# Spreading norms by transposes, and issuing 64-row products by turns, in a two-layer hybrid diffusion backbone

## The chip, the cores and the metric

The kernel runs on one core of one Trainium2 chip. The metric is the device time of one execution in microseconds (us), the median of the runs shown; lower is better. TensorE (PE) is the matrix engine, VectorE (DVE), ScalarE (ACT) and GpSimd (POOL) do the elementwise work, and SyncE (SP) issues the transfers. The profile is one execution taken by the hardware profiler.

## The reference, cut to what matters

Two layers; each is a feed-forward, a mixing sub-layer of two head groups (windowed attention and the RWKV-7 scan, run in both directions), and a second feed-forward. 512 latent tokens and 256 context tokens, 1024 channels, 8 + 8 heads of 64 channels, float32.

```python
def rms_norm(x, gain):
    xf = x.astype(jnp.float32)
    y = xf * lax.rsqrt(jnp.mean(xf * xf, axis=-1, keepdims=True) + RMS_EPS)
    return (y * gain.astype(jnp.float32)).astype(x.dtype)

def attn_heads(p, q_gain, k_gain):            # q and k: a norm per head
    q, k, v = jnp.split(p, 3, axis=-1)
    q = rms_norm(q.reshape(shape), q_gain) * ATTN_SCALE
    k = rms_norm(k.reshape(shape), k_gain)
    ...
def neighbourhood_attention(q, k, v, k_ctx, v_ctx, rel_bias):
    ...
        s_loc = jnp.einsum('bqhd,brwhd->bhqrw', q_i, k_i) + bias[None]
        s_ctx = jnp.einsum('bqhd,bchd->bhqc', q_i, k_ctx)
        p = jax.nn.softmax(jnp.concatenate([s_loc, s_ctx], axis=-1), axis=-1)
        # out = p_loc @ v_i + p_ctx @ v_ctx
def rwkv_prepare(p, ...):
    kk = heads(k * key_k)
    kk = kk * lax.rsqrt(jnp.maximum(jnp.sum(kk * kk, axis=-1, keepdims=True), L2_EPS))
    for d in range(2):
        w_log = -jax.nn.softplus(-(decay_w0[d] + jnp.tanh(dw) @ decay_w2[d])) - 0.5
        a = jax.nn.sigmoid(iclr_a0[d] + da @ iclr_a2[d])
        ...
# per layer: x += 0.5 g0 ffn(norm(x)); x += g1 mix(norm(x)); x += 0.5 g2 ffn(norm(x))
```

## The kernel before, in words

Channels lie on the 128 partitions, tokens along the free dimension. The feed-forwards (`up` L341, `accumulate` L423) are wide products on all 128 rows of TensorE. Each starts with `prep_end` (L283): the sums of squares of all tokens come out by tokens, and the reciprocal root (L294) is spread over the channels by six products of a broadcast column with the identity (L300), four tokens' tiles into one PSUM bank and two into a second; ACT copies each bank out as `rstd`.

The mixing sub-layer (`mix` L1096) is a set of streams, each a generator: the scan's chains, the solves, the blocks (`rwkv_blocks` with `rwkv_block` L780), the projections (`rkv` L655, `qkv` L469), in layer 0 the next layer's modulations (`mod` L170), the attentions (`attention` L515) and the output projection. `drive` (L71) takes their steps by turns: each `yield` gives a share of TensorE and a distance to the stream's next step, from the table `E` (L68). A planner then orders the instructions of each engine; it takes the ready one of the highest rank, and the ranks are chains, solves, blocks, then all the others, in the order in which `drive` issued them. On the chip each engine runs its instructions in that fixed order.

PSUM has eight banks, by tag (L65): two of `g` for the wide products and for the attention's scores and outputs, two of `p` for the RWKV preparation, two of `a` for the attention's transposes and the norms, one each for the chain and its outputs.

Per-head norms go through `head_rms` (L446), used for q, k and the scan's direction kk: the heads' sums (L451), a root and a reciprocal, a spreading along the free dimension on DVE (L460), and then four or six products with the identity (L465) that bring the result over the channels. DVE multiplies by it (L164, from L494 and L674).

`attention` takes a head pair: 6 blocks of 128 queries in layer 0 (the last two of the context), 4 in layer 1. A unit is one block and one head, and a head's 64 channels lie on one half of the rows. A step of the stream is the scores of unit n (L557, L560, or L542 for the context) into a `g` bank, DVE's evacuation with the bias and the maximum (L562), the exponential, and the transposes (L577, L575) of unit n - 2; after the second head of a block come the products with v (L598) and a copy out. So a head pair has 14 steps in layer 0 and 10 in layer 1. The score tiles have four places (tag `w2`).

In `rwkv_block`, run 12 times per layer, two lots of two 256-column products (L797) fill one `p` bank each: the decay's on rows 0 to 63, then the learning rate's on rows 64 to 127; ACT reads each bank through a tanh. The products `gt` (L856) of the preceding block use the same two banks.

Of the kernel before, what the change touches and what calls it, by code (L numbers as in the profile page):

```python
# [12 lines left out]
ALU = mybir.AluOpType  # L13
# [10 lines left out]
# half of the columns of the feed-forward's first product, even as the products ask for  # L24
# [4 lines left out]
# head pairs are scanned two at a time  # L29
# [10 lines left out]
# A chunk of 32 tokens of the RWKV scan is computed, per head and direction, on a state tile's columns X = [S; V; U] with S by channels,  # L40
# V and U by tokens, of its rows SR[e], VR[e] and UR[e], by a block of 128 columns: X's next S by channels, its outputs, and U from [S; V].
# A stage holds the blocks of a head pair's 4 chunks, by head, direction and chunk.
# [15 lines left out]
# SBUF tiles by tag: (floats per partition, tiles)  # L58
TAGS = dict(x=(2 * XH, 6), r=(2 * XH, 10), g3=(772, 3), z=(2 * XH, 3), k=(4 * XH, 2), sp=(520, 8), ob=(512, 4), ro=(256, 5),
            st=(SW, 8), w2=(512, 4), wr=(512, 3), q4=(1024, 3))  # L60
# The feed-forward's first product goes by Winograd's form of Strassen's algorithm: seven products of half the features, channels and tokens.
# The tags of the tiles that hold its right operands' 56 parts
PARTS = ("st",) * 3 + ("k",) * 2 + ("sp",) * 8 + ("ob",) * 4 + ("q4",) + ("z",) * 2 + ("x",) * 6 + ("r",) * 2
# PSUM banks by tag: GEMM, chain, chain's outputs, RWKV preparation, attention
BANKS = dict(g=2, ch=1, co=1, p=2, a=2)  # L65
OUTS = (0, 2, 4, 6)
# weights of the streams' steps (TensorE's share, distance to the stream's next step): they set the order of issue
# [3 lines left out]
def drive(tc, *streams):  # L71
    """Issues the steps of the streams, the first of them that is ready at a time, TensorE's use setting the clock.
    The scheduler prefers the streams in the order of their ranks."""
    now, live, first = 0.0, [[0.0, g, rank] for rank, g in streams], tc.cur_priority
    prio = {rank: first + rank * 200000 for rank, _ in streams}
    while live:
        for s in live:
            if s[0] > now:
                continue
            tc.cur_priority = prio[s[2]]  # L80
            step = next(s[1], "end")
            prio[s[2]] = tc.cur_priority
            if step == "end":
                live.remove(s)
                break
            if step is not None:
                s[0] = max(now + step[0], now + step[1])
                now += step[0]
                break
        else:  # L90
            now = max(now + 0.2, min((s[0] for s in live if s[0] > now), default=0.0))
    tc.cur_priority = max(prio.values())
# [14 lines left out]
class Net:  # L107
# [62 lines left out]
    def mod(self, l, i, tag, cols, bank):  # L170
# [3 lines left out]
        for c0 in range(0, KD * D, step):  # L174
# [6 lines left out]
            # the four column groups at once  # L181
# [71 lines left out]
    def prep_wino(self, kt, tag="g3"):  # L253
        """The right operands of k-tiles kt and kt + 4: x scaled, and twice the shifts."""
# [28 lines left out]
    def prep_end(self):  # L283
# [13 lines left out]
        for t0, hs in ((0, XLAT), (4, xctx))[:2 if self.prep_ctx else 1]:  # L297
            pb = self.bank("a", "rsps")
            for t in range((hs.stop - hs.start) // 128):
                nc.tensor.matmul(pb[:, 128 * t:128 * t + 128], lhsT=rs[:, t0 + t:t0 + t + 1].to_broadcast([128, 128]),  # L300
                                 rhs=self.c(C_ID), start=True, stop=True)
# [4 lines left out]
    def weight(self, src):  # L306
        """The parts of four tiles of weights: (high, low)."""
# [6 lines left out]
    def product(self, w, xh, xl, segs, banks="g"):  # L314
        """The product's segments one after the other: (columns, PSUM) as each is finished."""
# [25 lines left out]
    def up(self, raw, ctx, hh, hl):  # L341
        """A tile of the hidden features."""
# [80 lines left out]
    def accumulate(self, src, k0, n, hh, hl, ctx, gate, after, banks="g"):  # L423
        """Adds the gated product of input tiles k0 to k0 + n to x, two output tiles m and m + 4 at a time."""
# [13 lines left out]
    def residual(self, product, m, gate):  # L438
        """Adds the gated product to x."""
# [6 lines left out]
    def head_rms(self, sq, nt, mean, tag, bank):  # L446
        """1/sqrt of each head's sum (or mean) of squares, spread over that head's channels, in PSUM banks."""
# [14 lines left out]
        for t0 in range(0, nt, 4):  # L462
            pb = self.bank(bank, "hrb")
            for t in range(t0, min(t0 + 4, nt)):
                nc.tensor.matmul(pb[:, 128 * (t - t0):128 * (t - t0) + 128], lhsT=rs[:, 128 * t:128 * t + 128], rhs=self.c(C_ID), start=True, stop=True)  # L465
# [3 lines left out]
    def qkv(self, l, p, last):  # L469
        """q and k normalised, and v in the order of the windows' key groups, of head pair p, to DRAM."""  # L470
# [31 lines left out]
    def transposed_tiles(self, out, src):  # L502
        """The transposes of six tiles of 128 x 128."""
# [6 lines left out]
    # key groups of v by tokens, of 128: columns 8-23, 24-39, 40-55, 0-7 with 56-63 of all rows, then the context  # L510
    # of each block of 16 query columns: (first column, columns, groups of them, step) of its keys, and their groups of v (group, its first key)
# [3 lines left out]
    def attention(self, l, p, last):  # L515
# [10 lines left out]
        units = [(b, e) for b in range(4 if last else 6) for e in range(2)]  # L526
        nab, sbs, pbs = {}, {}, {}

        def slots(b):
            """(group of v, its keys, the first's column of the scores); blocks 4 and 5 are the context's."""  # L530
# [6 lines left out]
        def scores(b, e):  # L537
            rows = HALVES[e]
            nm = self.small("nm", [128, 1])
            if b > 3:  # L540
                ps = self.bank("g", "scc", (128, 256))
                nc.tensor.matmul(ps, lhsT=q[rows, 128 * b:128 * b + 128], rhs=k[rows, CTX], start=True, stop=True)  # L542
                nc.vector.tensor_reduce(out=nm, in_=ps, axis=AX.X, op=ALU.max, negate=True)
                sb = self.t("w2", "scs", 256)
                self.softmax(sb, ps, 1.0, nm)
                return sb
# [6 lines left out]
            ps = self.bank("g", "sc")  # L553
            lq = q[rows, 128 * b:128 * b + 128]
            o = 0
            for c0, n, g, step in self.KEYS[b]:
                nc.tensor.matmul(ps[:, o:o + 8 * n * g], lhsT=lq,  # L557
                                 rhs=free_ap(k[rows, c0:c0 + 1], [[step, g], [GW, 8], [1, n]]), start=True, stop=True)
                o += 8 * n * g
            nc.tensor.matmul(ps[:, 256:512], lhsT=lq, rhs=k[rows, CTX], start=True, stop=True)  # L560
            sb = self.t("w2", "sc", 512)
            nc.vector.tensor_tensor_reduce(out=sb.rearrange("p (a c) -> p a c", a=2),  # L562
                                           in0=ps.rearrange("p (a c) -> p a c", a=2),
                                           in1=free_ap(nab[y][:, e], [[256 * (2 - e), 2], [1, 256]]), scale=-1.0,
                                           scalar=3.0e38, op0=ALU.add, op1=ALU.min, accum_out=nm)
            self.softmax(sb, sb, -1.0, nm)
            return sb
# [18 lines left out]
        lag = 2  # L586
        for n in range(len(units) + lag):
            if n < len(units):
                sbs[units[n]] = scores(*units[n])
            if n >= lag:  # L590
                b, e = units[n - lag]
                pbs[e] = transposed(b, sbs.pop((b, e)))
                if e:
                    sl = slots(b)
                    pv = self.bank("g", "pv", (128, 128))
                    for s, (g, ks, _) in enumerate(sl):
                        for h, rows in enumerate(HALVES):
                            nc.tensor.matmul(pv[rows], lhsT=vt[ks, g, rows], rhs=pbs[h][ks, 128 * s:128 * s + 128],  # L598
                                             start=s == 0, stop=s == len(sl) - 1)
                    if b > 3:  # L600
                        self.act(out[:, 128 * b:128 * b + 128], pv, AF.Copy)
                    else:
                        self.act(out[:, LAT].rearrange("p (i b c) -> p b i c", b=4, c=16)[:, b], pv.rearrange("p (i c) -> p i c", c=16), AF.Copy)
            yield E["a"]
# [12 lines left out]
    def shifted(self, l, m, ctx):  # L617
        """Token-shifted projection tile m (14 of them), the context's tokens first: (tile, its column of token 0)."""
# [36 lines left out]
    def rkv(self, l, p, last):  # L655
        """r, k and k's direction of head pair p by blocks of 256 tokens, and v, to DRAM."""
# [40 lines left out]
    def span(b, d):  # L697
        """Tokens (context first) of block b of 256 in the order of direction d's scan."""
# [3 lines left out]
    def rwkv_bonus(self, l, p, b0, b1, g):  # L702
        """Sum over a head's channels of r (k_f + k_b) u, times v, of the blocks b0 to b1 of tokens."""
# [14 lines left out]
    def rwkv_blocks(self, l, i, last):  # L718
        """The blocks of group i of two head pairs, but for U's part in itself."""
# [26 lines left out]
    def rwkv_solves(self, l, i):  # L746
        """The inverses of group i, applied to the blocks' U rows."""
# [32 lines left out]
    def rwkv_block(self, l, p, b, emit, ltd, g):  # L780
        """Block b of 256 tokens of each direction's scan, with the backward direction's tokens reversed: two stages."""
# [9 lines left out]
        # tanh of half the decay's and of minus half the learning rate's argument  # L791
        th, tan = self.t("sp", "th", 512), self.t("sp", "tan", 512)
        for i, t in enumerate((th, tan)):
            rows = HALVES[i]
            ps = self.bank("p", "lz", (128, 2, 256))
            for d in range(2):
# [456 lines left out]
```

## Time and profile before

| | |
|---|---|
| median of 3 runs (3946.70, 3961.48, 3950.52) | 3950.52 us |
| span of the profiled execution | 3962.7 us |
| PE busy | 3659.5 us, 92% of the span |
| PE weight loads (beside PE) | 3152.3 us, 80% |
| DVE busy | 2934.9 us, 74% |
| ACT busy | 1498.9 us, 38% |
| POOL busy | 1005.3 us, 25% |
| mean granted TensorE clock | 0.926 of full speed |

The span is what the profiled execution took, 12.2 us (0.3%) over the median and 1.2 us over the longest of the three runs. A float32 product leaves two records on PE, a transpose one. Records of successive products overlap, so a merged row of n records is shorter than n times the time of one, and PE's busy time is the union of its records. A clock of 1.00 is 2.4 GHz, 0.50 is 1.2 GHz.

### The profile page before, as it was taken

The numbers are of one execution on the slowest core, as the hardware profiler recorded it, in microseconds if no ns is written. First come the engines' busy times: TensorE is split into PE (matmuls) and PEld (weight loads), VectorE is DVE, ScalarE is ACT, GpSimd is POOL, SyncE is SP. The second block draws the span as 40 slices with busy tenths as digits, with TensorE's granted clock in tenths as the row PEclk, the third lists the DMA queues.
The fourth block names the chain that finished last, engine by engine and source line by source line (L and its number), as shares of the span: only waits on it lengthen the run. The fifth ranks groups of instructions, "written<-read, shape, count | busy, mean of one in ns | idle before, by whom it ended". The sixth has DMA issues, their size and how long they took to land. (4 is left out here: it accounts for less than half of the span.)

```text
span 3962.7 us, 73554 instructions
## 1 busy us (share of the span) xinstructions
PE 3659.5 (92%) x28980; PEld 3152.3 (80%) x28980; DVE 2934.9 (74%) x5682; ACT 1498.9 (38%) x2968; POOL 1005.3 (25%) x1156
## 2 busy tenths in 40 slices
PE   6999999999799899799999999999998977878988
PEld 4788889878666567699998999998886756768888
DVE  5666678575868766788878888886668686768888
ACT  4232224343444432533335433334434442243333
POOL 2222222020312311322323322230203131133333
PEclk8999999989899779799999999999998885779999
DMA  5333332332245243111121111123322210212222
GB/s 194 123 118 108 107 107 73 102 95 76 69 151 173 90 150 111 66 67 64 65 75 54 65 64 67 66 71 115 108 88 73 68 60 18 70 59 94 82 82 94
DMA packets 229849, 354.62 MB, mean 89 GB/s; under 512 B 47744, under 2 KB 156672, under 8 KB 217216
## 3 DMA queue, kind: packets, MB, share of 16 engines
q1 hardware_dynamic: 229504, 349.92, 26.9%
q8 instruction: 229, 3.75, 0.4%
q14 instruction: 116, 0.95, 0.1%
HBM read 306.31 MB, written 43.52 MB: 88 GB/s over the span
## 5 line engine op out<-in xcount | busy, mean ns | idle before, releaser
L364 PE MATMUL mw<-b,wq 128*128 128x386 f32 (+1 forms) x4224 | 783.4, 329 | 15.5 <-ACT wq L167 9.0
L364 PEld LDWEIGHTS mw<-b,wq 128*128 128x128 f32 x4224 | 701.8, 191 | 40.4 <-ACT wq L167 11.6
L322 PE MATMUL mm<-h,whi 128*128 128x256 f32 (+1 forms) x2816 | 669.9, 331 | 22.1 <-ACT h L167 20.1
L164 DVE SCALAR_TENSOR_TENSOR x<-mm,mods,x 128x256 f32<-128x256 f32 (+1 forms) x768 | 418.0, 573 | 192.8 <-PE mm L322 188.8
L322 PEld LDWEIGHTS mm<-h,whi 128*128 128x128 f32 x2816 | 475.4, 191 | 99.0 <-ACT h L167 23.5
L364 PE MATMUL mw<-b,whi 128*128 128x386 f32 (+1 forms) x2112 | 520.6, 329 | 30.4 <-ACT b L167 11.8
L322 PE MATMUL mm<-h,wlo 128*128 128x256 f32 (+1 forms) x1408 | 450.2, 328 | 2.0 <-DVE wlo L161 1.9
L364 PEld LDWEIGHTS mw<-b,whi 128*128 128x128 f32 x2112 | 373.8, 190 | 40.3 <-ACT b L167 16.0
L167 ACT ACTIVATE whi<-wraw 128x512 fp32r<-128x512 f32 x312 | 196.1, 629 | 493.4 <-PE mm L322 297.1
L364 PE MATMUL mw<-b,wlo 128*128 128x386 f32 (+1 forms) x1056 | 346.6, 328 | 1.1 <-DVE wlo L161 0.8
L167 ACT ACTIVATE wq<-raw 128x512 fp32r<-128x512 f32 x352 | 219.6, 628 | 338.3 <-PE mw L364 264.7
L161 DVE TENSOR_TENSOR wq<-raw,wq 128x512 fp32r<-128x512 f32 x352 | 292.4, 832 | 68.2 <-ACT wq L167 65.3
L322 PEld LDWEIGHTS mm<-h,wlo 128*128 128x128 f32 x1408 | 268.6, 192 | 28.5 <-DVE wlo L161 2.8
L161 DVE TENSOR_TENSOR wlo<-wraw,whi 128x512 fp32r<-128x512 f32 x312 | 222.3, 714 | 54.1 <-ACT whi L167 38.0
L161 DVE TENSOR_TENSOR up_g<-up_g,mw 128x386 f32<-128x386 f32 (+1 forms) x352 | 182.3, 518 | 92.2 <-PE mw L364 75.5
L161 POOL TENSOR_TENSOR raw<-raw,s 128x512 f32<-128x512 f32 x88 | 125.7, 1428 | 432.1 <-DVE wq L161 429.5
L161 POOL TENSOR_TENSOR s<-raw 128x512 f32<-128x512 f32 x88 | 125.2, 1423 | 432.5 <-DVE wlo L161 371.4
L167 ACT ACTIVATE whi<-s 128x512 fp32r<-128x512 f32 x176 | 110.5, 629 | 321.0 <-PE mm L322 229.3
L322 PE MATMUL mm<-x,whi 128*128 128x258 f32 (+2 forms) x832 | 207.5, 335 | 0.0
L364 PEld LDWEIGHTS mw<-b,wlo 128*128 128x128 f32 x1056 | 201.1, 190 | 3.2 <-DVE wlo L161 2.4
L184 PE MATMUL modps<-wmod,cs 128*32 128x256 f32 x1152 | 172.7, 427 | 23.6 <-DMA wmod<-in_w_mod_dram 22.9
L161 POOL TENSOR_TENSOR up_g<-up_g,rstd 128x386 f32<-128x386 f32 (+1 forms) x88 | 103.5, 1176 | 342.8 <-DVE up_g L161 337.9
(226 smaller groups left out, 7043.5 us busy)
## 6 DMA issues: line engine op xcount, KB each, us to landing
raw<-in_ffn_up_dram SPq DMA_DIRECT2D x88, 1024.0 KB, 5.4
wraw<-in_ffn_down_dram SPq DMA_DIRECT2D x176, 256.0 KB, 3.1
wmod<-in_w_mod_dram SPq DMA_DIRECT2D x144, 256.0 KB, 3.1
wmod<-in_w_mod_dram SPq DMA_DIRECT2D x224, 128.0 KB, 2.2
wraw<-in_w_in_dram SPq DMA_DIRECT2D x104, 256.0 KB, 2.8
wmod<-in_w_mod_dram SPq DMA_DIRECT2D x8, 1024.0 KB, 10.9
wraw<-in_w_out_dram SPq DMA_DIRECT2D x32, 256.0 KB, 3.1
in<-rkv SPq DMA_DIRECT2D x20, 384.0 KB, 3.9
```

Of the source, the lines that this page charges most:

```text
L161: (eng or self.nc.vector).tensor_tensor(out=out, in0=a, in1=b, op=op)
L164: self.nc.vector.scalar_tensor_tensor(out=out, in0=a, scalar=s, in1=b, op0=op0, op1=op1)
L167: self.nc.scalar.activation(out, in_, f, **kw)
L184: nc.tensor.matmul(ps[q:q + 32], lhsT=self.cs[:, kt], rhs=w, start=kt == 0, stop=kt == KD - 1)
L322: nc.tensor.matmul(ps, lhsT=wt, rhs=xt[k][:, c0:c1], start=k == 0 and n == 0, stop=k == nk - 1 and n == 2)
L364: nc.tensor.matmul(ps, lhsT=wt[:, c], rhs=self.bs[i][k][xt], start=k == 0 and m == 0, stop=k == 3 and m == 2)
```

## The change

Three edits. The products with the identity that spread norms (L300, L465) become transposes of the same operand. In `attention` a step is now the scores of both heads of a block, with the matrix products by turns for the two halves of the rows, into both `g` banks; or the transposes of both heads of the preceding block with their products with v. A head pair has 12 steps in layer 0 and 8 in layer 1, of the same weights. In `rwkv_block` the four products with `lora` are issued by turns for the halves, so that both `p` banks are taken before the first tanh. Comments are dropped.

```diff
             for t in range((hs.stop - hs.start) // 128):
-                nc.tensor.matmul(pb[:, 128 * t:128 * t + 128], lhsT=rs[:, t0 + t:t0 + t + 1].to_broadcast([128, 128]),
-                                 rhs=self.c(C_ID), start=True, stop=True)
+                nc.tensor.transpose(pb[:, 128 * t:128 * t + 128], rs[:, t0 + t:t0 + t + 1].to_broadcast([128, 128]), self.c(C_ID))
...
             for t in range(t0, min(t0 + 4, nt)):
-                nc.tensor.matmul(pb[:, 128 * (t - t0):128 * (t - t0) + 128], lhsT=rs[:, 128 * t:128 * t + 128], rhs=self.c(C_ID), start=True, stop=True)
+                nc.tensor.transpose(pb[:, 128 * (t - t0):128 * (t - t0) + 128], rs[:, 128 * t:128 * t + 128], self.c(C_ID))
...
-        def scores(b, e):
-            rows = HALVES[e]
-            nm = self.small("nm", [128, 1])
+        def scores(b):
+
+            nms = [self.small("nm", [128, 1]) for _ in HALVES]
             if b > 3:
-                ps = self.bank("g", "scc", (128, 256))
-                nc.tensor.matmul(ps, lhsT=q[rows, 128 * b:128 * b + 128], rhs=k[rows, CTX], start=True, stop=True)
...
+                pss = [self.bank("g", "scc", (128, 256)) for _ in HALVES]
+                for rows, ps in zip(HALVES, pss):
+                    nc.tensor.matmul(ps, lhsT=q[rows, 128 * b:128 * b + 128], rhs=k[rows, CTX], start=True, stop=True)
+                for e, (ps, nm) in enumerate(zip(pss, nms)):
+                    nc.vector.tensor_reduce(out=nm, in_=ps, axis=AX.X, op=ALU.max, negate=True)
...
-            ps = self.bank("g", "sc")
-            lq = q[rows, 128 * b:128 * b + 128]
+            pss = [self.bank("g", "sc") for _ in HALVES]
             o = 0
             for c0, n, g, step in self.KEYS[b]:
-                nc.tensor.matmul(ps[:, o:o + 8 * n * g], lhsT=lq,
-                                 rhs=free_ap(k[rows, c0:c0 + 1], [[step, g], [GW, 8], [1, n]]), start=True, stop=True)
+                for rows, ps in zip(HALVES, pss):
+                    nc.tensor.matmul(ps[:, o:o + 8 * n * g], lhsT=q[rows, 128 * b:128 * b + 128],
+                                     rhs=free_ap(k[rows, c0:c0 + 1], [[step, g], [GW, 8], [1, n]]), start=True, stop=True)
                 o += 8 * n * g
-            nc.tensor.matmul(ps[:, 256:512], lhsT=lq, rhs=k[rows, CTX], start=True, stop=True)
...
+            for rows, ps in zip(HALVES, pss):
+                nc.tensor.matmul(ps[:, 256:512], lhsT=q[rows, 128 * b:128 * b + 128], rhs=k[rows, CTX], start=True, stop=True)
+            for e, (ps, nm) in enumerate(zip(pss, nms)):
+                sb = self.t("w2", "sc", 512)
...
-        lag = 2
-        for n in range(len(units) + lag):
-            if n < len(units):
-                sbs[units[n]] = scores(*units[n])
-            if n >= lag:
-                b, e = units[n - lag]
-                pbs[e] = transposed(b, sbs.pop((b, e)))
-                if e:
...
+        nb = 4 if last else 6
+        for n in range(nb + 1):
+            if n < nb:
+                scores(n)
+                yield E["a"]
+            if n:
+                b = n - 1
+                pbs = [transposed(b, sbs.pop((b, e))) for e in range(2)]
+                sl = slots(b)
+                pv = self.bank("g", "pv", (128, 128))
...
+                yield E["a"]
...
-        for i, t in enumerate((th, tan)):
-            rows = HALVES[i]
-            ps = self.bank("p", "lz", (128, 2, 256))
-            for d in range(2):
+        pss = [self.bank("p", "lz", (128, 2, 256)) for _ in HALVES]
+        for d in range(2):
+            for rows, ps in zip(HALVES, pss):
                 nc.tensor.matmul(ps[:, d], lhsT=lora[rows, d], rhs=self.zin[rows, spans[d]], start=True, stop=True)
+        for i, (t, ps) in enumerate(zip((th, tan), pss)):
             for d in range(2):
                 n = 8 * i + 4 * d + p
                 self.act(t[:, 256 * d:256 * d + 256], order(ps[:, d], d), AF.Tanh, scale=0.5 - i, bias=self.rv[:, n:n + 1])
```

## Rows read from the trace of the kernel before

**Rows 1.** The page: span, and busy time of each engine (share, instructions).

```profile
span 3962.7 us, 73554 instructions
PE 3659.5 (92%) x28980; PEld 3152.3 (80%) x28980; DVE 2934.9 (74%) x5682; ACT 1498.9 (38%) x2968; POOL 1005.3 (25%) x1156
```

**Rows 2.** Mixing's stages: length, busy (count) PE, PEld, DVE, ACT, POOL; clock, DMA, GB/s.

```profile
700.00:1050.00 350.00, 325.91 (x2576) 278.29 (x2574) 226.54 (x465) 129.07 (x239) 54.77 (x108) 0.93 0.29 90
1100.00:1280.00 180.00, 178.15 (x2315) 118.54 (x2312) 136.31 (x358) 81.97 (x209) 35.93 (x66) 0.98 0.53 167
2740.00:3010.00 270.00, 256.26 (x2269) 223.14 (x2268) 185.87 (x382) 112.92 (x215) 46.53 (x95) 0.98 0.32 100
3018.00:3235.00 217.00, 188.19 (x2341) 143.35 (x2340) 166.36 (x420) 95.68 (x243) 53.66 (x97) 0.84 0.19 61
3240.00:3515.00 275.00, 218.02 (x2800) 178.98 (x2797) 178.24 (x385) 82.40 (x181) 55.50 (x98) 0.69 0.17 52
```

**Rows 3.** Busy time of the products with the identity, all stages: L465, then L300.

```profile
sum 3963.00, PE 45.81 PEld 41.04; mean PE 5.73 PEld 5.13
sum 3963.00, PE 13.49 PEld 12.66; mean PE 1.69 PEld 1.58
```

**Rows 4.** Timeline, PE: six transposes, and six products with the identity (start, us, what).

```profile
737.99 0.82 PE L973 MATMUL vt<-consts,sh 128*128 128x128 f32 x6
786.57 1.50 PE L465 MATMUL hrb<-consts,hrs 128*128 128x128 f32 x12
```

**Rows 5.** Timeline around one spreading of a head's norm, PE and DVE.

```profile
724.84 0.56 DVE L460 TENSOR_SCALAR hrs<-hsda 128x768 f32<-128x768 f32 x1
725.55 2.90 PE L465 MATMUL hrb<-consts,hrs 128*128 128x128 f32 x12 [1.83 <-DVE hrs L460]
727.64 1.33 DVE L164 SCALAR_TENSOR_TENSOR kk<-sh,rv,hrb 128x512 f32<-128x512 f32 x2 [2.23 <-PE hrb L465]
728.89 1.02 DVE L161 TENSOR_TENSOR pin<-mm,rstd 128x512 f32<-128x512 f32 x2
729.63 0.79 PE L322 MATMUL mm<-xh,whi 128*128 128x512 f32 x1 [1.18 <-DVE pin L161]
```

**Rows 6.** Timeline, PE: scores of one head and the next head's start; context scores, pair and single.

```profile
1158.62 0.71 PE L557 MATMUL sc<-kt,qt 64*128 64x128 f32 x4
1159.16 0.59 PE L560 MATMUL sc<-kt,qt 64*128 64x256 f32 x2
1159.69 0.63 PE L184 MATMUL modps<-wmod,cs 128*32 128x256 f32 x4
1164.97 0.49 PE L557 MATMUL sc<-kt,qt 64*128 64x128 f32 x2
...
1280.63 0.70 PE L542 MATMUL scc<-kt,qt 64*128 64x256 f32 x4
...
1284.53 0.70 PE L542 MATMUL scc<-kt,qt 64*128 64x256 f32 x2
```

**Rows 7.** DVE's evacuation of a score bank, all 64 (ns min/median/max).

```profile
L562 DVE CUSTOM_DVE_ANT_1 sc<-sc,nab x32: 643/691/693, 1059.6 to 3208.9; 128x512 f32<-128x512 f32 x32
L562 DVE DVE_READ_ACCUMULATOR2_ANT nm<- x64: 73/83/122, 1060.2 to 3223.7; 128x1 f32 x64
```

**Rows 8.** Timeline: `rwkv_block`'s products, both halves together, then two halves apart.

```profile
876.06 1.14 PE L797 MATMUL lz<-zin,lora 64*128 64x256 f32 x8
...
811.37 1.13 PE L797 MATMUL lz<-zin,lora 64*128 64x256 f32 x4
813.78 0.41 DVE L161 TENSOR_TENSOR st<-gt,consts 64x256 f32<-64x256 f32 x1
816.90 1.13 PE L797 MATMUL lz<-zin,lora 64*128 64x256 f32 x4
```

**Rows 9.** Stretches around transposes and around Rows 5: the same columns as Rows 2.

```profile
736.00:742.00 6.00, 6.00 (x46) 5.68 (x45) 1.86 (x4) 2.21 (x5) 0.00 (x0) 1.00 0.19 31
724.50:734.80 10.30, 8.07 (x24) 6.74 (x25) 5.75 (x11) 1.17 (x3) 0.27 (x4) 0.50 0.19 64
```

More of the change, by code (lines that the diff above doesn't have):

```diff
@@ L525, in attention @@
         out = self.t("x", f"att{p}", T)
-        units = [(b, e) for b in range(4 if last else 6) for e in range(2)]
-        nab, sbs, pbs = {}, {}, {}
+        nab, sbs = {}, {}
         def slots(b):
@@ L535, in slots @@
             return [(4, full, 256), (5, full, 384), (g0, full, 0), (g1, slice(k1, k1 + 64) if g1 == 3 else full, 128)]
-        def scores(b, e):
-            rows = HALVES[e]
-            nm = self.small("nm", [128, 1])
+        def scores(b):
+            nms = [self.small("nm", [128, 1]) for _ in HALVES]
             if b > 3:
-                ps = self.bank("g", "scc", (128, 256))
-                nc.tensor.matmul(ps, lhsT=q[rows, 128 * b:128 * b + 128], rhs=k[rows, CTX], start=True, stop=True)
[L543 to L546, printed above, removed]
+                pss = [self.bank("g", "scc", (128, 256)) for _ in HALVES]
[3 more added lines that the diff above has]
+                    nc.vector.tensor_reduce(out=nm, in_=ps, axis=AX.X, op=ALU.max, negate=True)
+                    sbs[b, e] = self.t("w2", "scs", 256)
+                    self.softmax(sbs[b, e], ps, 1.0, nm)
+                return
             y = (0, 1, 1, 2)[b]
@@ L552, in scores @@
                 nab[y] = t
-            ps = self.bank("g", "sc")
-            lq = q[rows, 128 * b:128 * b + 128]
+            pss = [self.bank("g", "sc") for _ in HALVES]
             o = 0
             for c0, n, g, step in self.KEYS[b]:
-                nc.tensor.matmul(ps[:, o:o + 8 * n * g], lhsT=lq,
-                                 rhs=free_ap(k[rows, c0:c0 + 1], [[step, g], [GW, 8], [1, n]]), start=True, stop=True)
+                for rows, ps in zip(HALVES, pss):
+                    nc.tensor.matmul(ps[:, o:o + 8 * n * g], lhsT=q[rows, 128 * b:128 * b + 128],
+                                     rhs=free_ap(k[rows, c0:c0 + 1], [[step, g], [GW, 8], [1, n]]), start=True, stop=True)
                 o += 8 * n * g
-            nc.tensor.matmul(ps[:, 256:512], lhsT=lq, rhs=k[rows, CTX], start=True, stop=True)
[L561 to L567, printed above, removed]
+            for rows, ps in zip(HALVES, pss):
+                nc.tensor.matmul(ps[:, 256:512], lhsT=q[rows, 128 * b:128 * b + 128], rhs=k[rows, CTX], start=True, stop=True)
+            for e, (ps, nm) in enumerate(zip(pss, nms)):
+                sb = self.t("w2", "sc", 512)
+                nc.vector.tensor_tensor_reduce(out=sb.rearrange("p (a c) -> p a c", a=2),
+                                               in0=ps.rearrange("p (a c) -> p a c", a=2),
+                                               in1=free_ap(nab[y][:, e], [[256 * (2 - e), 2], [1, 256]]), scale=-1.0,
+                                               scalar=3.0e38, op0=ALU.add, op1=ALU.min, accum_out=nm)
+                self.softmax(sb, sb, -1.0, nm)
+                sbs[b, e] = sb
         def transposed(b, sb):
@@ L584, in transposed @@
             return pb
-        lag = 2
-        for n in range(len(units) + lag):
-            if n < len(units):
-                sbs[units[n]] = scores(*units[n])
-            if n >= lag:
-                b, e = units[n - lag]
-                pbs[e] = transposed(b, sbs.pop((b, e)))
-                if e:
[L594 to L604, printed above, removed]
+        nb = 4 if last else 6
[8 more added lines that the diff above has]
+                pv = self.bank("g", "pv", (128, 128))
+                for s, (g, ks, _) in enumerate(sl):
+                    for h, rows in enumerate(HALVES):
+                        nc.tensor.matmul(pv[rows], lhsT=vt[ks, g, rows], rhs=pbs[h][ks, 128 * s:128 * s + 128],
+                                         start=s == 0, stop=s == len(sl) - 1)
+                if b > 3:
+                    self.act(out[:, 128 * b:128 * b + 128], pv, AF.Copy)
+                else:
+                    self.act(out[:, LAT].rearrange("p (i b c) -> p b i c", b=4, c=16)[:, b], pv.rearrange("p (i c) -> p i c", c=16), AF.Copy)
+                yield E["a"]
         nc.sync.dma_start(out=self.yd[p][:, 0:NL if last else T], in_=out[:, 0:NL if last else T])
```

## The prediction, made before the changed kernel ran

> **What bounds the kernel now.** First the page's busy times: PE is busy for 92% of the span, DVE for 74% [rows 1]. That is an average, so next the stretches of the mixing sub-layers, where nearly all of the changed code runs [rows 2]. The reader is to see PE's busy column against the length. While the projections run (700 to 1050 us in layer 0, 2740 to 3010 in layer 1) PE works 93 and 95% of the time. In the middle of layer 0's attentions (1100 to 1280) it works 178 of 180 us at a clock of 0.98: time taken off PE there is time off the end. Layer 1's attentions (3018 to 3235) are looser, 188 of 217 us at 0.84, and in the tail behind them (3240 to 3515) PE has 218 of 275 us at 0.69: there the scan's chain and what feeds it set the pace, and little of PE's saving comes through. So the question is how much PE time each edit frees, and in which of these stretches.
>
> **The norms.** The products that spread the norms are 136 (L465) and 34 (L300), and PE is busy with them for 45.81 + 13.49 = 59.30 us [rows 3]. Six of them at full clock take 1.50 us, six transposes of the same size 0.82 us [rows 4]: one record instead of two. At 0.82/1.50 = 0.547 the 59.30 us become 32.4, which frees 26.9 us. Part runs at half clock: 170/6 groups at 1.50 us would be 42.5 us, so the 59.30 say that some 40% do, and one such group takes 2.90 us [rows 5]. I let the ratio hold there too.
>
> Is it on the path? [rows 5] show the ring: PE waits 1.83 us for the spread roots, multiplies for 2.90 us, DVE's two multiplications wait for that (2.23 us idle), DVE then evacuates the projection's two banks (1.02 us), and PE, 1.18 us idle, goes on. What is taken off the group is taken off PE's next start. DVE needs only the first bank, four of the six, to begin, so the lower end is 26.9 x 4/6 = 18; the upper end is all 26.9. I take 23, since PE is over 93% busy in these stretches and idles right behind the group where it idles at all. The feed-forwards' six groups stand alone at a sub-layer's start and count in full.
>
> The Trainium skill (TensorE: Matmul & The Clock Gate, Terms) puts the transpose mode of this chip at 4 times as fast for float32. By it 44.5 of the 59.30 us would go instead of 26.9; [rows 4] show 1.8 times, and the rows decide.
>
> **Scores by turns.** The scores of one head of a latent block hold PE from 1158.62 to 1159.69, 1.07 us [rows 6]. What a pair costs, the trace shows on the context's scores: two records take 0.70 us, and four, of two heads that happened to come together, also 0.70 [rows 6]. The halves of the rows work side by side, and the second head is free. There are 4 blocks x 4 head pairs x 2 layers = 32 latent pairs and 2 x 4 = 8 context pairs: at most 32 x 1.07 + 8 x 0.70 = 39.8 us.
>
> A pair needs both `g` banks free at once. In layer 0 the next head's scores come 6.35 us after the first's (1158.62, 1164.97) [rows 6], while DVE empties a bank in 0.69 + 0.08 us [rows 7]: the attention is last in rank there, and when its turn comes both banks are free. I take three quarters of 16 x 1.07 + 8 x 0.70 = 22.7 us, 17. In layer 1 PE has time, so scores are issued as soon as one bank is free, and DVE frees the two 0.77 us apart: a third of 17.1, 6. Not all reaches the end: 0.85 in layer 0, whose later attentions also run beside solves, and 188/217 = 0.87 less what the tail takes back, say 0.75, in layer 1. That is 14.5 + 4.5 = 19. The ends are 0 and 39.8.
>
> **The block's products by turns.** Both halves together take 1.14 us, one half alone 1.13 [rows 8], so a pairing saves one half's PE time, the 1.07 us of the same four records in the scores. Of 24 calls three already stand together like the first of these rows, so at most 21 x 1.07 = 22.5 us. But [rows 8] also show why the others stand apart: between the first half (811.37) and the second (816.90) DVE still empties a bank of the preceding `gt` (813.78), and both use `p`. The edit takes no bank away from `gt`; with one bank free the planner will put the first half's two products out and hold the second's, as now. I take one call in six, 3 us; the ends are 0 and 22.5. Nothing is queued behind a wait here that wasn't before: the first tanh now comes behind four products instead of two, which at a pairing is the same moment.
>
> **The attention's steps.** 96 steps become 80 of the same weight, so the attentions get ahead of the modulations and the output projection in the last rank. The transposes of a block's second head move behind both heads' scores. Both heads' score tiles now take all four `w2` places when two blocks are under way; before, it was three. No row prices this; the work is the same and the order of the ranks stays, so I set it at 0 and keep 15 us either way, about one block of layer 1 (217 us over 16 blocks, 13.6 us) [rows 2].
>
> **The sum.** 23 + 19 + 3 = 45 us off the profiled 3962.7 leave 3917.7. The median stands at 3950.52/3962.7 = 0.9969 of that span, so 3906 us, 1.1% less.
>
> **The rivals.**
>
> *The pairs don't meet.* The edit orders the calls, but banks come free one at a time in the attentions as they do for `gt`, and the planner keeps the halves apart. Then only the norms' 23 us go: 3939.7 x 0.9969 = 3928 us. For it speaks [rows 8], against it the 6.35 us between heads [rows 6].
>
> *Everything meets and everything is on the path.* 26.9 + 39.8 + 22.5 = 89 us: 3862 us. Against it speak [rows 8] and the loose stretches of layer 1 [rows 2].
>
> *The attention waits for its own banks (slower).* Place: layer 1's 16 blocks. A pair holds both `g` banks until DVE has emptied both, 2 x 0.77 = 1.54 us [rows 7], and without modulations to fill it PE idles: 25 us. Idle PE also lowers the clock: if this stretch fell from 0.84 to the 0.69 of the one behind it, PE's 188 us there would grow by 188 x (0.84/0.69 - 1) = 41 us [rows 2]. With the norms' 23 taken off that is +43 us: 3993 us. It decides from the point where less than 1.5 us of other PE work is ready per block. Against it: a block takes 13.6 us there, and chain, blocks and solves share them.
>
> *The clock falls with the transposes.* Low clock costs as much as anything here: around [rows 5] it was 0.50 for 10.3 us, of which PE was busy 8.07 [rows 9], some 4 us lost. If each of the 60% of 30 groups that run at full clock now, 18, brought one such stretch, 72 us would be lost against 45 gained: 3977 us. The trace speaks against it: around six transposes at 738 us the clock was 1.00 [rows 9]. The rule stands in the Trainium skill (TensorE: Matmul & The Clock Gate, Part 4: PE-mode transpose): a transpose is not counted as PE activity as a product is. By that rule these groups would count for nothing; so far the trace does not show it.
>
> **How the numbers follow.** The forecast, half to three quarters of the pairs and the norms, gets 0.48 (3885 to 3928); pairs that don't meet 0.18; everything 0.12; the bank wait 0.09; the clock 0.05; a new order that eats most of the gain without any of these, 0.08. A difference of 0.5%, 3930.8 to 3970.3 us, is about what a measurement of this kernel can tell from no change. Faster by more than that: 0.48 + 0.12 + a little over half of the 0.18, 0.70. Within: the rest of the 0.18, the 0.08, and mild forms of the two slow cases, 0.19. Slower: 0.11. The range is 3866 to 3958: it leaves out about half of the best case and most of the two slow ones.
>
> **What would show it.** The norms: L465 and L300 with one record per product, six in 0.82 us at full clock, busy time near 32 us, and PE's start behind [rows 5] about a microsecond sooner. The pairs: merged rows of both heads' scores in some 1.1 us, often in layer 0, seldom in layer 1. The blocks: most L797 rows still of four records. Wrong would be: a longer stretch of layer 1's attentions with PE waiting for the score evacuations; a lower clock in the projections' stretches; or PE time freed as said and the tail of layer 1 longer by the same.

## The result: the changed kernel is slower

The changed kernel takes 3984.36 us (median), the kernel before 3952.8 us beside it: a ratio of 1.0077, interval [1.0055, 1.0099]. The forecast was 3906 us, 3866 to 3958. TensorE is busy for less time than before [rows 1], and yet the span is longer. The page of after:

```profile
span 3982.1 us, 73220 instructions
PE 3640.1 (91%) x28810; PEld 3126.8 (79%) x28810; DVE 2940.2 (74%) x5682; ACT 1507.1 (38%) x2972; POOL 1007.3 (25%) x1156
```

First the edits' own rows. The norms' transposes, L464 and L300, answer to [rows 3]: 24.14 + 7.31 = 31.45 us busy where the products took 59.30.

```profile
sum 4000.00, PE 24.14 PEld 17.77; mean PE 24.14 PEld 17.77
sum 4000.00, PE 7.31 PEld 5.73; mean PE 7.31 PEld 5.73
```

The scores, three heads in a row and then the one pair of a latent block that runs wholly side by side (timeline, PE; start, us, what), answer to [rows 6]. These heads are as far apart as before, 5 to 6 us. The two heads' score products leave 176 pairs of records in the whole trace, and nine pairs of records start side by side, within 40 ns; before, eight did.

```profile
1098.52 0.70 PE L557 MATMUL sc<-kt,qt 64*128 64x256 f32 x2
1099.06 0.59 PE L561 MATMUL sc<-kt,qt 64*128 64x256 f32 x2
1103.68 0.71 PE L557 MATMUL sc<-kt,qt 64*128 64x128 f32 x4
1104.23 0.59 PE L561 MATMUL sc<-kt,qt 64*128 64x256 f32 x2
1110.05 0.71 PE L557 MATMUL sc<-kt,qt 64*128 64x128 f32 x4
...
1151.72 0.71 PE L557 MATMUL sc<-kt,qt 64*128 64x256 f32 x4 [1.45 <-DVE nm L564]
```

Then the stages, cut at events that both kernels have: the first spreading of the mixing's norm, the first score, the next sub-layer's spreading, and for layer 1 the last two of these. Before, then after; columns as in [rows 2]:

```profile
683.00:1055.00 372.00, 344.44 (x2659) 294.48 (x2660) 239.54 (x486) 136.62 (x251) 59.70 (x120) 0.92 0.28 87
1055.00:1657.00 602.00, 536.57 (x6209) 380.13 (x6208) 422.86 (x970) 250.66 (x581) 145.37 (x229) 0.85 0.38 121
3018.00:3561.00 543.00, 440.25 (x5317) 351.63 (x5317) 386.52 (x877) 206.52 (x493) 130.13 (x214) 0.75 0.18 56
```

```profile
681.00:1040.00 359.00, 331.58 (x2586) 280.50 (x2584) 238.02 (x483) 139.80 (x252) 56.65 (x112) 0.93 0.30 90
1040.00:1671.00 631.00, 540.25 (x6206) 382.40 (x6205) 429.16 (x972) 253.32 (x584) 149.34 (x236) 0.84 0.37 115
3030.00:3577.00 547.00, 439.64 (x5317) 346.82 (x5317) 390.82 (x883) 207.52 (x492) 132.06 (x220) 0.76 0.18 55
```

Layer 0's projections are 13 us shorter, and the attentions with the mixing's end 29 us longer, at the same work: 6206 records for 6209, 540 us of PE for 537. So 26 of the 29 us are idle time of PE, 91 us where it was 65. The rest is within 4 us a stage. So the question is what holds layer 0's end.

Its last steps, before and then after: the last two modulations' transposes (`modpt`, two each), the second half of the scan's readings (`pj`), the chain's last products (`ch`), and the next sub-layer's norm (`rsps`). Each row ends with the first and the last start:

```profile
L189 PE MATMUL modpt<-consts,modsb x4: 270/272/274, 1505.2 to 1548.5; 128*128 128x128 f32 x4
L996 PE MATMUL pj<-ob,consts x12: 378/379/483, 1508.9 to 1588.7; 128*128 128x256 f32 x12
L938 PE MATMUL ch<-k,st x128: 218/219/316, 1480.4 to 1572.3; 96*32 96x64 f32 x64, 128*32 128x64 f32 x64
L300 PE MATMUL rsps<-consts,rs x12: 394/421/422, 1657.2 to 1659.5; 128*128 128x128 f32 x12
```

```profile
L189 PE MATMUL modpt<-consts,modsb x4: 270/272/329, 1541.9 to 1578.6; 128*128 128x128 f32 x4
L998 PE MATMUL pj<-ob,consts x12: 379/483/694, 1544.4 to 1604.7; 128*128 128x256 f32 x12
L940 PE MATMUL ch<-k,st x126: 217/219/316, 1488.1 to 1575.7; 128*32 128x64 f32 x64, 96*32 96x64 f32 x62
L300 PE MATMUL rsps<-consts,rs x6: 415/417/417, 1670.8 to 1671.8; 128*128 128x128 f32 x6
```

The chain ends at nearly the same time, 1572 and 1576. The readings begin 2 to 4 us behind the next-to-last modulation, at 1509 and 1544. Before, the last reading starts 16 us behind the chain; after, 29 us, which is 63 behind that modulation and 26 behind the last modulation. The norm follows the last reading by 66 to 69 us. In both programs the reading takes the very bank of `a` that `modpt` gives back, while the last modulation's `modps` holds the other, so the first two readings go through a single bank. The third starts 1 us behind the last modulation (timeline, PE; before, then after):

```profile
1548.37 0.38 PE L189 MATMUL modpt<-consts,modsb 128*128 128x128 f32 x2
1549.49 0.70 PE L996 MATMUL pj<-ob,consts 128*128 128x256 f32 x2
...
1578.45 0.38 PE L189 MATMUL modpt<-consts,modsb 128*128 128x128 f32 x2
1579.77 0.70 PE L998 MATMUL pj<-ob,consts 128*128 128x256 f32 x2
```

### The profile page after: what moved, and what is told of

Its sections match the earlier page's. It is cut to its first block, busy times and chain, and to the rows that moved or that the text cites. A ratio compares the mean times of both kernels' runs of the same rounds, so it can differ in the third digit from the quotient of the medians.

```text
span 3982.1 us, 73220 instructions
## 1 busy us (share of the span) xinstructions
PE 3640.1 (91%) x28810; PEld 3126.8 (79%) x28810; DVE 2940.2 (74%) x5682; ACT 1507.1 (38%) x2972; POOL 1007.3 (25%) x1156
```

## The experiments

**The edits one at a time.** e1 has the two transposes alone, e2 `attention` alone, e3 `rwkv_block` alone (all parts of the diff above), e4 the first and the third. Three theories stood: A, the attentions' new steps cost the time; B, transposes lower the clock; C, the mixing's end is bound by the scan, and each edit makes the planner deal the order anew, for 8 to 15 us either way.

> Only the 170 products that spread norms become transposes; attention and block as before. Theory A (the attention's new steps cost the time): this edit alone gains what it gained in layer 0's projections, 15 to 25 us, about 3930 us. Theory B (the transposes lower the clock, as the low time of 31 us instead of 14 between 2700 and 3020 us suggests): slower than before by 5 to 20 us, with about 30 us of low clock in layer 1's projections. Theory C (the mixing is bound by the scan's chain and every new plan comes out a little differently): within 8 us of before.

> Only the attention's steps are changed. Theory A: slower than before by 30 to 50 us, some 3990 us, with the last modulation at about 1575 us instead of 1548 and the scan's last readings of layer 0 behind it. Theory B: within 8 us of before. Theory C: within 15 us of before either way.

> Only the four products with lora are issued by turns. Theories A and B: within 8 us of before, 4 more of the 24 calls paired, 4 us less PE time. Theory C: within 15 us either way, whatever PE time is saved.

> Norms and block edits, the attention as before. Theory A: 20 to 28 us faster than before, about 3927 us: the changed kernel without its costly part. Theory B: slower than before by 5 to 20 us. Theory C: within 15 us of before, and not the sum of the two edits alone.

Measured: e1 3977.89 us, ratio 1.0066 [1.0041, 1.0092]; e2 3995.81, 1.0101 [1.0078, 1.0123]; e3 3997.69, 1.0099 [1.0067, 1.0130]; e4 3978.55, 1.0065 [1.0036, 1.0094]. Every edit alone is slower, and they don't add up. A falls with e1 and e3, which don't touch the attentions, though its 3990 us for e2 came near; B falls with e2 and e3, which have no new transpose. C missed its sizes: 21 to 41 us where it gave 8 to 15. In all four kernels the next-to-last modulation ends later than before (1506 us): at 1527, 1556, 1538 and 1547, and the norm comes at 1669, 1687, 1677 and 1690, for 1657. The end of layer 0 in e2, rows as above:

```profile
L189 PE MATMUL modpt<-consts,modsb x6: 272/328/476, 1479.7 to 1555.7; 128*128 128x128 f32 x6
L999 PE MATMUL pj<-ob,consts x12: 378/557/695, 1559.3 to 1617.4; 128*128 128x256 f32 x12
L300 PE MATMUL rsps<-consts,rs x12: 274/418/421, 1686.9 to 1688.9; 128*128 128x128 f32 x12
```

The first of these rows ends with the next-to-last modulation: again the readings follow it at once, 50 us later than before.

**The order against the instructions.** e5 lets the planner see the products and turns the 170 into transposes once the order is set; e6 is the reverse. The order of every engine's instructions in e5 is that of the kernel before, in e6 that of e1.

```diff
     with tile.TileContext(nc, schedule_with_timeline_sim=True) as tc:
         tile_hybrid_kernel(tc, *args)
+    as_transposes(nc)    # e5: matmul "hrb", "rsps" -> is_transpose=True, in place
+    as_products(nc)      # e6, on e1: the reverse
```

> The 170 products that spread the norms become transposes only after the planner has set the order, so every engine's instructions stand in the order of the kernel before, and nothing else differs. Theory O (the order costs, the instructions save): layer 0's projection stage is about 12 us shorter, as it was with the norms alone (360 after 372), a few us more at places where TensorE sets the end, layer 0's end is not longer (195): 3930 to 3948 us, against 3957 before. Theory T (the transposes themselves cost, by the clock or by a wait behind them): as with the norms planned anew, 3970 to 3985.

> The reverse: the planner sees transposes and sets the order of the norms-only kernel, then they are turned back into the products of the kernel before, so the instructions are those of the kernel before in another order. Theory O: the norms-only kernel's 3978 us and what the transposes saved there, 3985 to 4000; layer 0's last modulations end near 1530 and 1570 us or later instead of 1505 and 1548, and its end is as long as there (225). Theory T: the time of the kernel before, 3950 to 3965.

e5 took 3945.18 us, 0.9961 [0.9945, 0.9976], and is the fastest kernel here; e6 took 3986.83, 1.0087 [1.0056, 1.0118]. With the kernel before (3960.97 beside these two) and e1 (3977.89, beside 3956.99) that is a square. The transposes save 16 us in the old order, and the new order costs 26 us with the products; both are clear of the noise. The other two sides compare kernels of two sets of runs: the new order costs 33 us with the transposes by the medians and 42 by the ratios, and in the new order the transposes save 9 or 8 us, which the intervals of e1 and e6 do not tell from nothing. Theory O holds and T falls. Layer 0's two stages, e5 and then e6 (whose profiled execution took 4009 us, 23 over its median):

```profile
682.00:1041.00 359.00, 329.24 (x2581) 278.31 (x2580) 237.90 (x484) 136.39 (x250) 59.08 (x118) 0.94 0.30 90
1041.00:1644.00 603.00, 535.23 (x6206) 379.85 (x6206) 422.78 (x971) 250.23 (x581) 146.13 (x230) 0.86 0.38 121
```

```profile
682.00:1044.00 362.00, 335.04 (x2661) 286.56 (x2662) 239.57 (x484) 140.11 (x252) 55.42 (x112) 0.96 0.30 89
1044.00:1686.00 642.00, 558.85 (x6205) 389.99 (x6205) 426.63 (x971) 251.68 (x582) 148.34 (x236) 0.82 0.36 113
```

In e5 the transposes' gain in the projections stays (359 us, then 603 as before); in e6 the same instructions as before take 642 us for 602, and its readings begin at 1547.2, behind a modulation that ends at 1543.7. Its projections, with the old products, take 362 us at a clock of 0.96, where they took 372 at 0.92. So the changed kernel's 13 us there need not be the transposes': another order gave 10 without them. Over all kernels whose readings use `a`, the stage takes 362 to 372 us with the products (six kernels) and 358 to 361 with the transposes (seven).

**The modulations' place.** e7 is the changed kernel with layer 1's modulations ranked ahead of the attentions; e8 is the kernel before with a rank of their own for them, e11 the kernel before with them ranked first, and e5's turn to transposes.

```diff
-mods = [] if last else [(3, self.fillers(l + 1, ...))]
+mods = [] if last else [(2, self.fillers(l + 1, ...))]   # e7; e11: 0; e8: 3, with projections, attentions and outs at 4
```

> The changed kernel with layer 1's modulations ranked ahead of the attentions for the planner (rank 2 for 3), which puts the last of them in TensorE's order back to where they stood in the kernel before. Theory G (layer 0's end waits for the modulations to give up a bank of a, for the last readings of the scan): the next-to-last modulation ends 15 to 35 us sooner than at 1542, the readings follow it within 5 us, layer 0's end falls from 209 to 180 to 197 us, and the whole to 3955 to 3975. Rival (the end follows something else in the new order): readings as late as before the edit, 1544 us, and 3978 to 3995 us.

> The kernel before, with layer 1's modulations given a rank of their own between the blocks of the scan and the attentions: no instruction is added or removed, the order is new, and the last modulations stand nearly where they stood. Theory G (a new order costs as far as it moves the modulations back): they stand some 40% as far back as in the norms-only kernel, where they ended 21 us later, so about 8 us more: 3957 to 3970. Rival (this order was fitted, any other costs the same): 3975 to 3995.

> The kernel before with layer 1's modulations ranked first for the planner, level with the scan's chain, which moves their last parts ahead in TensorE's order by more than any other kernel here; then the products that spread the norms become transposes in their places, as in e5. Theory G: the next-to-last modulation ends 20 to 40 us sooner than the 1493 us of e5, the readings follow within 5 us, and the whole is 3910 to 3935 us, faster than e5's 3945. Rival (the readings then wait for the chain, which the modulations hold up): layer 0's end as in e5, 3940 to 3955.

e7: 3975.16 us, 1.0053 [1.003, 1.0075], 9 us less than the changed kernel by the medians, with intervals that overlap, and at the upper edge of what theory G gave.

```profile
L189 PE MATMUL modpt<-consts,modsb x4: 272/272/328, 1504.1 to 1550.2; 128*128 128x128 f32 x4
L998 PE MATMUL pj<-ob,consts x12: 377/380/694, 1507.2 to 1587.7; 128*128 128x256 f32 x12
L940 PE MATMUL ch<-k,st x126: 219/219/244, 1488.8 to 1571.2; 128*32 128x64 f32 x64, 96*32 96x64 f32 x62
L300 PE MATMUL rsps<-consts,rs x6: 272/272/273, 1657.5 to 1658.1; 128*128 128x128 f32 x6
```

The modulation is back at 1504, the readings at 1507, and the norm comes at 1657.5 for 1670.8. So the bank is worth up to 13 us; the chain, which ends 4 us sooner too, may have a part in them. But 1657 is also the kernel before's time, although e7's projections ended 15 us sooner: now the chain sets the end, 1571 and 16 us more.

e8, another order with the modulations almost in place: 3961.79 us, 1.0011 [0.9991, 1.0031]; the next-to-last modulation ended 13 us later than before, the norm came 5 later. So a new order need not cost anything that can be measured; as far as these runs go, it costs where it moves something that the end waits for. e11: 3987.14 us, 1.0074 [1.0057, 1.009], a miss. Its next-to-last modulation ended at 1487 and the readings began at 1490.5, but the products that open the last blocks of the scan (`bops`) ended 31 us later than before, and the chain with them:

```profile
L714 PE MATMUL bops<-ts,consts x4: 592/644/697, 1488.1 to 1493.4; 128*128 128x512 f32 x4
L938 PE MATMUL ch<-k,st x192: 217/219/244, 1485.4 to 1592.7; 128*32 128x64 f32 x96, 96*32 96x64 f32 x96
L996 PE MATMUL pj<-ob,consts x12: 377/379/692, 1490.5 to 1607.1; 128*128 128x256 f32 x12
```

**Without the modulations.** Both kernels, without layer 1's modulations, so that layer 1 takes layer 0's in their place:

```diff
-mods = [] if last else [(3, self.fillers(l + 1, ...))]
+mods = []     # and self.mods[1] = self.mods[0], gs likewise
```

> The kernel before without layer 1's modulations (layer 1 takes layer 0's in their place), so 80 us of products, their loads and their hold on a bank of a are gone from layer 0's mixing; all else is computed. Theory G (layer 0's end waits for the modulations): the readings of the scan's second half start as soon as the chain is there, attentions and end together fall from 602 us to 520 to 575, the whole to 3880 to 3930. Rival (the scan's chain sets the end by itself, the modulations only lie beside it): 590 to 602 us there, 3945 to 3960.

> The changed kernel without layer 1's modulations, in the same way. Theory G: with the gate away the two kernels differ by what the edits save; layer 0's projections stay 13 us shorter, attentions and end come to within 10 us of the kernel before without modulations, and the whole is 5 to 20 us faster than that one. Rival A (the attentions' new steps cost time by themselves, whatever the modulations do): attentions and end are 15 to 30 us longer than in that one, and the whole 5 to 25 us slower.

e9: 3966.76 us, 1.0034 [1.0016, 1.0053]; e10: 3959.87, 1.0011 [0.9993, 1.0029]. For the size of e9 theory G was wrong: 80 us of products gone, and nothing gained. Its rival, the chain by itself, came nearer: 609 us for the attentions and end where it gave 590 to 602. e9's readings and chain, e10's, then the two stages of layer 0's attentions and end, and the two of layer 1, e9 first:

```profile
L996 PE MATMUL pj<-ob,consts x12: 377/379/694, 1430.9 to 1586.7; 128*128 128x256 f32 x12
L938 PE MATMUL ch<-k,st x166: 219/219/243, 1479.8 to 1572.3; 96*32 96x64 f32 x83, 128*32 128x64 f32 x83
```

```profile
L998 PE MATMUL pj<-ob,consts x12: 377/378/483, 1419.8 to 1575.4; 128*128 128x256 f32 x12
L940 PE MATMUL ch<-k,st x128: 219/219/315, 1494.3 to 1560.7; 96*32 96x64 f32 x64, 128*32 128x64 f32 x64
```

```profile
1049.00:1658.00 609.00, 504.27 (x5615) 383.39 (x5615) 419.72 (x948) 252.07 (x584) 141.13 (x229) 0.78 0.19 57
3026.00:3556.00 530.00, 425.65 (x5319) 338.32 (x5320) 381.57 (x877) 207.31 (x493) 132.19 (x214) 0.79 0.18 57
```

```profile
1039.00:1643.00 604.00, 514.57 (x5612) 391.22 (x5611) 424.83 (x949) 249.84 (x583) 147.74 (x236) 0.78 0.18 58
3004.00:3565.00 561.00, 462.71 (x5320) 363.75 (x5319) 391.54 (x884) 206.95 (x492) 131.85 (x220) 0.73 0.17 54
```

The readings begin 78 us sooner, so they had waited for the bank; but the last of them still comes 14 us behind the chain, in both. So layer 0's end is the later of two, the chain and the modulation's bank, and in the kernel before the two lay side by side. With the bank out of it the changed kernel is ahead: layer 0 ends at 1643 for 1658, 10 of the 15 us from its projections (358 us for 368) and 5 behind them. On the whole it is 7 us ahead by the medians, with intervals that overlap; the profiled executions say 8 behind, because layer 1 ran at a clock of 0.73 in one and 0.79 in the other, 561 us for 530, with the same records but one. Rival A falls here too.

**The readings' banks.** The cleanest cut seemed to give the readings banks that the attentions have left:

```diff
-pj = self.bank("a", "pj", (128, 2, 2, 64))      # pt2, pg likewise
+pj = self.bank("g", "pj", (128, 2, 2, 64))
```

> The changed kernel with the banks of the scan's readings taken from g, which the attentions have left by then, instead of a, where they stand behind the modulations' tiles. Theory G2 (layer 0's end is the later of two: the scan's chain, and the bank that the next-to-last modulation gives back to the readings): the readings of the second half start before the next-to-last modulation ends (1542 us), the last one comes 12 to 18 us after the last product of the chain (1576), layer 0's end is 180 to 197 us instead of 209, the whole 3960 to 3976. Rival (the readings follow something else): no change, 3978 to 3992.

> The kernel before with the readings' banks from g. Theory G2: its readings end 16 us after the chain already, so both limits fall together and nothing but the chain is left: 3945 to 3965, the same as before within 0.3%, and about 10 to 30 us faster than the changed kernel's own version of this. Rival (banks alone set the end): 3925 to 3945.

> The kernel with the attentions' edit alone (3996 us, its next-to-last modulation ended at 1556) with the readings' banks from g. Theory G2: the next norm's first product comes at 1655 to 1665 us instead of 1687, the whole 3965 to 3980. Rival (the attentions' new steps cost by themselves): 1675 to 1690, 3985 to 4000.

> The kernel with the low-rank products by turns alone (3998 us, its next-to-last modulation ended at 1538) with the readings' banks from g. Theory G2: the next norm's first product comes at 1648 to 1662 us instead of 1677, the whole 3970 to 3984, with the 10 us that its layer 1 was longer at a low clock still in it or not. Rival (these products by turns cost by themselves): 1670 to 1680, 3988 to 4002.

All missed: 4011.77 us, 1.0131 [1.0093, 1.017]; 4014.57, 1.0134 [1.0106, 1.0162]; 4023.56, 1.0164 [1.0127, 1.02]; 4027.55, 1.018 [1.0132, 1.0227]. `g` is also the bank of the projections, whose stage grew to 410 us in e13 and 402 in e12 as other work moved into it (2986 and 2906 records, 2659 before), and of the output projection, behind which the last four readings now stand. In e12, readings and then chain:

```profile
L998 PE MATMUL pj<-ob,consts x8: 379/632/695, 1601.6 to 1624.0; 128*128 128x256 f32 x8
L940 PE MATMUL ch<-k,st x128: 217/219/315, 1486.7 to 1554.7; 96*32 96x64 f32 x64, 128*32 128x64 f32 x64
```

The four begin 47 us behind a chain that is there at 1555, and the last of them starts 69 behind it. The wait was moved, not removed, so these four say little about the bank of `a`. The two whole kernels come out level, 4012 and 4015, as they would if a third thing held both. Why e14 and e15 are 9 and 13 us behind e13 stays open.

## Why the prediction was wrong, point by point

*The attention's steps, at 0 ± 15: the step that failed.* It said that the work is the same and the order of the ranks stays, and so put the cost of a new order at nothing, here and in the other terms. The ranks stay, but the planner picks among ready instructions by its own estimate of their times, and each edit alone changed what it picked: the next-to-last modulation of layer 0's end came 21 to 50 us later. What the runs showed in its place: e6, the instructions of the kernel before in the order that the norms' edit brings, takes 26 us more, and the attentions' edit alone (e2) 39. In the changed kernel the last two modulations start 37 and 30 us later, the readings wait for the bank that they hold, and layer 0's attentions and end take 29 us more. The rival "a new order" had a chance of 0.08 and no price of its own, so the range ended at 3958.

*"Time taken off PE there is time off the end": failed.* I read it from PE's 178 of 180 us [rows 2]. e9 left out the modulations' 80 us of products: in layer 0's attentions and end PE's busy time fell by 33 us, its idle time rose from 65 to 105, and the stage became 7 us longer. A busy engine isn't the bound when the end waits for a chain of latencies or for a bank: those two were not looked for.

*The norms, 23 us.* The PE time was right: 27.9 us freed (26.9 forecast). On the path it is 16 us in e5 (9 to 22 by its interval); 9 in the new order, within the noise. The term was mis-sized: the lower end, 18, was nearer. That layer 0's end and layer 1 wait for more than PE would explain it; this is argued, not shown.

*Scores by turns, 19 us: failed at "when its turn comes both banks are free".* Nine pairs of records side by side for eight; busy time of the scores went up, from 99.1 to 107.0 us. In the order written for TensorE the halves of 38 of the 40 pairs stay apart (in four places a block's second head stands beside the next block's first instead), often by the preceding block's value products, which use the same bank, and by ready work of higher rank. "The pairs don't meet" was right about this, not about the time.

*The block's products, 3 us: right in PE time.* Seven calls together for three, 55.95 to 52.26 us busy. With this edit alone (e3) the whole kernel is 41 us slower.

*The rivals.* The slower one that I gave, 3993 us, names a time near the measured one, but not its mechanism: layer 1's attentions were shorter, not longer (first score to the end of the last block 202 us, 223 before), and layer 1 as a whole took 547 for 543. "The clock falls with the transposes": in layer 0's projections the clock is 0.94 in e5 and 0.92 before, but in layer 1's it is 0.95 for 0.98 (before, then e5; columns as in [rows 2]):

```profile
2708.00:3018.00 310.00, 292.12 (x2497) 255.55 (x2497) 212.02 (x431) 126.14 (x235) 54.86 (x114) 0.98 0.31 97
2695.00:3007.00 312.00, 290.66 (x2427) 252.67 (x2427) 210.74 (x428) 125.92 (x235) 53.75 (x111) 0.95 0.32 96
```

So one place of two shows a fall, and it goes with 2 us, not with the 72 of this rival. e6 has 0.95 there too, with the products in the other order, so the transposes need not be its cause. By the Trainium skill (TensorE: Matmul & The Clock Gate, Part 4: PE-mode transpose) a transpose does not count as PE activity as a product does; the one place agrees with that and the other does not.

*Where the changed kernel's 19 us (profile) are:* −13 in layer 0's projections, +29 in its attentions and end, of which 13 to 15 at most are the modulation's bank (e7; the last reading at 1604.7 for 1576 + 14) and the rest the 13 us of head start that the scan did not use: its last `bops` start at 1462 in both, and its chain ends at 1572 and 1576. This rest is argued, and why the planner puts those blocks no sooner wasn't tried. +4 in layer 1, −1 elsewhere.

## What to carry to other kernels

When a planner orders the instructions by its own estimates, an edit has two effects, the instructions' and the new order's, and the second can be larger; measure them apart by planning with one form and running with the other. Before counting freed engine time as time, follow the stage's end back to its last releaser (a bank, a chain), and look for the second limit that lies just behind it. Writing two products next to each other in the source does not put them next to each other in the queue.

## What the runs showed of the hardware that was not expected

With work taken off TensorE, its clock was lower. In the kernel before, the modulations' products took it 80 us of layer 0's attentions and end (busy PE, PEld, DVE):

```profile
1055.00:1657.00 602.00, 79.91 (x576) 20.74 (x576) 3.80 (x9) 0.85 0.38 121
```

Without them (e9) PE's busy time there fell from 537 to 504 us, not by 80. Part of their time had run beside other products: in the kernel before, the 5615 records that are not the modulations' cover 481 us, and the same number in e9 504. The granted clock of the stage fell from 0.85 to 0.78 (0.84 to 0.78 from the changed kernel to e10), and the time was 609 us for 602. In layer 1, whose stage has 5317 to 5320 records in the five kernels named here, the length goes with the clock from one kernel's profile to the next: 530 us at 0.79 (e9), 534 at 0.77 (e5), 543 and 547 at 0.75 and 0.76 (before and after), 561 at 0.73 (e10). PE is idle for 98 to 107 us of it in all five, so the difference lies in its busy time. A difference of 10 us there in one profiled execution is not yet the change's; why the clock differs stays open.

A product with the identity is two records of 273 to 275 ns at full clock (e6's `rsps`, twelve, below), a transpose one of 272 (e7's, six, above): half the records, each as long as before, and over the whole kernel 59.30 us for 31.45, 1.9 times. The factor of 4 for float32 of the Trainium skill (TensorE: Matmul & The Clock Gate, Terms) is not what these rows show.

```profile
L300 PE MATMUL rsps<-consts,rs x12: 273/275/275, 1686.4 to 1687.6; 128*128 128x128 f32 x12
```
